# The S5 layer's parameter tables in a decoder trunk: products moved from GpSimd to VectorE, without the zero half, with 16 angles in place of 64

## The chip, the core and the metric

The kernel runs on one core of a Trainium2 chip. The metric is device time in microseconds (us), the median of the runs. Engines are named as in the profile: PE (TensorE, PEld is its weight load), DVE (VectorE), ACT (ScalarE), POOL (GpSimd), SP (SyncE, which only starts transfers here).

## What is computed

A trunk of two layers on 256 tokens of 1024 channels. Each layer is a SwiGLU feed-forward with a layer norm, a token mixer with a layer norm, a second feed-forward with a layer norm, and a gated embedding. The mixer of the first layer holds an S5 recurrence, and the change is in what is prepared for it:

```
lam_bar = jnp.exp(lam * dt)
b_bar = ((lam_bar - 1.0) / lam)[..., None] * lax.complex(b_re, b_im)
bu = jnp.einsum('blgp,gnp->blgn', ug, b_bar)
_, states = lax.associative_scan(linear_recurrence_combine, (a, bu), axis=1)
y = jnp.real(jnp.einsum('blgn,gpn->blgp', states, c)) + d_skip * ug
```

There are 64 groups of 16 channels, with 64 complex states each.

## The kernel before

**Feed-forward.** Four feed-forward blocks run, named f00, f01, f10 and f11. Each takes 11 chunks of 256 hidden columns. Weights come as units of 1 MB (wst, two buffers, started by SP). ACT casts each half of a unit to float32r (wh, L61), DVE subtracts to get the rest (wl, L63), and PE multiplies three times: x high with wh, x high with wl, x low with wh (L71 to L73). For a chunk, gate and up go into gu_f; ACT applies SiLU (sg_f, L204), DVE multiplies (L205), PE transposes (ht_f, L208), ACT and DVE split the result (hh_f L211, hl_f L212), and PE multiplies down into acc_f. At the end DVE starts the layer norm (r_ln, L124).

**S5 parameters.** They are computed during f00, in hooks between its chunks (`params`, L1308), from weights alone. First `s5_scalars` makes small tables of powers of the eigenvalue (s5lq, s5le, 128x32 each). Then there are eight batches of four pairs of groups. Two groups share the 128 partitions, 64 states each. The loaded B and C (s5m) have 32 columns for a pair, and half of them are zero, so that a product of the matrix with both groups' channels keeps the groups apart. A batch (`s5_params`):

- loads s5m, 256 KB;
- DVE makes B times its factor (s5tv, s5e, 6 operations of 128x128);
- POOL makes the products with three powers for E (6 operations of 128x384) and four powers for Q (6 of 128x512, into the packed tile s5pk);
- DVE and ACT make cosine and sine of 64 angles for each of 4 pairs (s5x, s5y: DVE 11 operations of 128x256, ACT two Sin);
- POOL starts the transfer of s5pk to DRAM (s5d);
- one hook later, in `rest`, PE transposes E (s5w, 8 transposes) and multiplies E with C (s5k, 16 matmuls), ACT copies both into s5pe and makes six block copies, DVE adds the skip weights (s5dd), POOL clears part of s5pe, and starts its transfer.

s5pk, s5pe and s5e have two buffers each. The mixer behind f00 reads all of it back from DRAM.

**Order.** Each engine runs its own queue in order. The order within a queue is made at build time by a scheduler that has its own estimates of durations; no table written by hand sets it. An instruction that waits holds up all behind it on its engine.

Of the kernel before, what the change touches and what calls it, by code (L numbers as in the profile page):

```python
# [114 lines left out]
def layer_norm(g, n, t, acc, coef, xT):  # L115
    """LN(ALPHA * x + ALPHA * coef * acc) of one token tile, from the scaled sum x + coef * acc."""
# [44 lines left out]
def run_tiles(g, ps, xT, tile_major=False):  # L161
    """x @ w for the next 512 columns of weights into one accumulator a token tile."""
# [22 lines left out]
def ffn(g, name, ln, hooks=None):  # L185
    """SwiGLU, accumulated over chunks of 256 hidden columns, and the LN behind it."""
# [62 lines left out]
def ple_proj(g, i, pT):  # L249
    """p[i] @ ple_w_proj[i]."""  # L250
# [22 lines left out]
def ple(g, i, pp, out):  # L273
    """x + sigmoid(x @ ple_w_gate[i]) * pp; the last layer's goes out."""
# [64 lines left out]
def s5_scalars(g):  # L339
    """What every state of the S5 layer needs: B's factor, powers of the discrete eigenvalue, its phase over  # L340
    four steps as a fraction of a turn in two parts, and its decay over four steps."""
# [5 lines left out]
    LE = g.s5c.tile([P, 2, 3, 32], F32, tag="le", name="s5le")  # L347
# [85 lines left out]
def s5_params(g, b):  # L433
# [72 lines left out]
    def rest():  # L506
        pk = g.s5p.tile([P, PACK_PE], F32, tag="s5pe", name=f"s5pe_{b}", bufs=2)
        W = pk[:, 0:1024].rearrange("p (a q c) -> p a q c", a=2, q=NP)
        T = pk[:, 1024:1536].rearrange("p (q c) -> p q c", q=NP)
        for i in range(2):  # L510
            tp = g.ps.tile([P, NP, P], F32, tag="tr", name=f"s5w_{b}_{i}", bufs=2)
            for q in range(NP):
                nc.tensor.transpose(tp[:, q, :], E[:, i, q, :], g.ident)
            nc.scalar.copy(W[:, i], tp)
        kp = g.ps.tile([P, NP, 32], F32, tag="tr", name=f"s5k_{b}", bufs=2)
        for q in range(NP):
            nc.tensor.matmul(kp[:, q, :], E[:, 0, q, :], Cr[:, q, :], start=True, stop=False)
            nc.tensor.matmul(kp[:, q, :], E[:, 1, q, :], nCi[:, q, :], start=False, stop=True)
        nc.gpsimd.memset(T, 0.0)
        nc.scalar.copy(T[:, :, 96:128], kp)  # L520
# [8 lines left out]
        nc.gpsimd.dma_start(g.s5dram[b][:, 0:PACK_PE], pk)  # L529
# [4 lines left out]
def project(g, name, tile_major=False):  # L534
    """x @ w for the next 512 columns: one accumulator a token tile."""
# [5 lines left out]
def narrow_project(g, pool, src, name, tag=None):  # L541
    """A [1024, 16] product by channel: rows 0-15 and 16-31 of the result sum to it."""
# [20 lines left out]
def to_channels(g, src, cts, out_ps):  # L563
    """Transposes [tokens, channels] tiles: out_ps[:, i, :] holds channel tile cts[i] for all tokens."""
# [5 lines left out]
def softplus_terms(g, v, shape, pool, name):  # L570
    """log1p(exp(-|v|)) of a small tile, accurate for small results too."""
# [17 lines left out]
def s5_inputs(g, pool, U, c):  # L589
    """Half of u, laid out [(4 steps, 2 groups, 16 channels), pair of groups, 64 chunks of steps]."""  # L590
# [28 lines left out]
def s5_batch(g, pool, U, G, b):  # L619
    """Four pairs of groups: states at the ends of chunks of four steps by a scan in the rotating frame, then  # L620
    the outputs."""
# [19 lines left out]
    def turn(src, name, out, ops):  # L641
        """The products with cos and sin, and out = (c0 op s1, c1 op s0)."""
# [22 lines left out]
def s5_half_out(g, G, c, yh, yl):  # L665
    """GELU of half of the channels, by channel, and its parts."""
# [22 lines left out]
def s5_outputs(g, pool, yT, yh, yl):  # L689
    """The gated outputs by channel, in two parts."""  # L690
# [788 lines left out]
```

## Time and profile before

| | us |
|---|---|
| runs of the kernel, median (lowest to highest) | 1315.52 (1308.86 to 1315.69) |
| profiled execution, first to last instruction (its span, the only time given of it) | 1321.4 |
| f00, from its first matmul to the first layer norm operation | 254.3 |
| f01 and f10, the same stretch | 180.3 each |

The profiled execution's span is 5.9 us above the median of the runs, which don't carry the profiler. A stage's row gives the stretch, its length, and then the busy time and the count of instructions of PE, PEld, DVE, ACT and POOL; PEclk is the granted clock of PE, 1.00 being 2.4 GHz and 0.50 being 1.2 GHz. A group's row gives count, busy time, mean duration, and behind the second bar the idle time just before them with what ended it. Durations of neighbours on one engine overlap by some 0.05 us, since the next starts before the last has written back; busy time counts an overlap once.

### The profile page before, as it was taken

What the parts mean: (1) busy time and instruction counts of PE and PEld (TensorE: products, weight loads), DVE (VectorE), ACT (ScalarE), POOL (GpSimd) and SP (SyncE); (2) the same over time, 40 slices, a digit from 0 to 9 for tenths busy, and PEclk for the clock granted to TensorE, in tenths of its full rate; (3) what the DMA queues carried; (4) which work ended last, traced back from release to release, by engine and by line L of the source; (5) the groups of instructions that cost most, each with busy time, mean ns of one, the idle gap of its engine ahead of it and who ended that gap; (6) DMA issues with size and microseconds to landing.
All of it is one profiled execution on the core that took longest, in us unless ns stands there. A gap on an engine that the chain in (4) does not pass through costs nothing.

```text
span 1321.4 us, 15959 instructions
## 1 busy us (share of the span) xinstructions
PE 1243.2 (94%) x6026; PEld 1024.8 (78%) x6026; DVE 887.9 (67%) x1230; ACT 625.5 (47%) x965; POOL 382.2 (29%) x307
## 2 busy tenths in 40 slices
PE   7899887999989799999999999999889999999998
PEld 6677666877878687788888788888667787888886
DVE  6999797577875875655557655555649867555566
ACT  6445444456454653444453554444355544444434
POOL 0557776544536652000000000000366650000000
PEclk9899898999998899999999999999988999999999
DMA  7556546765753144655563655555443135655542
GB/s 277 173 201 229 179 182 229 276 231 168 258 193 138 59 142 159 230 197 182 190 216 105 250 191 191 191 182 201 146 131 124 65 135 177 209 188 191 191 159 96
DMA packets 39932, 238.98 MB, mean 181 GB/s; under 512 B 4624, under 2 KB 5296, under 8 KB 16176
## 3 DMA queue, kind: packets, MB, share of 16 engines
q1 hardware_dynamic: 30960, 206.58, 44.9%
q10 hardware_dynamic: 5952, 15.66, 3.3%
q0 software_dynamic: 2944, 15.73, 3.1%
q8 instruction: 47, 0.77, 0.2%
q14 instruction: 29, 0.24, 0.1%
HBM read 223.27 MB, written 14.68 MB: 180 GB/s over the span
## 4 chain that ended last, share of the span: by engine, by line
PE 61%; DVE 19%; DMA 7%; POOL 5%; issue 4%; ACT 4%; ACTq 0%; DVEq 0%; POOLq 0%; SPq 0%
PE gu_f L73 9%; PE gu_f L72 9%; PE gu_f L71 9%; DVE wl L63 5%; PE acc_f L71 5%; PE acc_f L73 5%; PE acc_f L72 5%; DMA wst<-in_wall_dram 4%; DMA s5m<-in_s5bc_dram 2%; ACT wh L61 2%; PE ht_f L208 1%; PE acc_ab L73 1%; PE acc_ab L71 1%; PE acc_ab L72 1%; POOL wl L63 1%
## 5 line engine op out<-in xcount | busy, mean ns | idle before, releaser
L63 DVE TENSOR_TENSOR wl<-wst,wh 128x1024 fp32r<-128x1024 f32 (+1 forms) x332 | 424.3, 1293 | 279.6 <-ACT wh L61 272.3
L61 ACT CAST wh<-wst 128x1024 fp32r<-128x1024 f32 (+1 forms) x378 | 386.0, 1045 | 309.8 <-PE gu_f L73 101.6
L63 POOL TENSOR_TENSOR wl<-wst,wh 128x1024 fp32r<-128x1024 f32 x46 | 120.5, 2621 | 310.7 <-ACT wh L61 310.7
L73 PE MATMUL acc_f<-wh,hl_f 128*128 128x512 f32 x352 | 140.0, 402 | 12.9 <-DVE hl_f L212 12.9
L71 PE MATMUL acc_f<-wh,hh_f 128*128 128x512 f32 x352 | 139.8, 398 | 3.7 <-ACT hh_f L211 3.6
L72 PE MATMUL acc_f<-wl,hh_f 128*128 128x512 f32 x352 | 140.0, 398 | 0.0
L82 POOL TENSOR_TENSOR rs_r_ln<-rs_w_ln,mhalf 128x1 f32<-128x1 f32 x12 | 11.3, 944 | 425.5 <-DVE rs_w_ln L80 425.5
L73 PEld LDWEIGHTS acc_f<-wh,hl_f 128*128 128x128 f32 x352 | 68.0, 193 | 29.7 <-DVE hl_f L212 15.6
L71 PEld LDWEIGHTS acc_f<-wh,hh_f 128*128 128x128 f32 x352 | 67.5, 192 | 18.6 <-ACT hh_f L211 5.0
L71 PE MATMUL gu_f<-wh,xh_in 128*128 128x512 f32 x176 | 73.1, 420 | 8.0 <-ACT wh L61 6.1
L72 PEld LDWEIGHTS acc_f<-wl,hh_f 128*128 128x128 f32 x352 | 67.5, 192 | 14.0
L73 PE MATMUL gu_f<-wh,xl_in 128*128 128x512 f32 x176 | 72.4, 411 | 0.0
L72 PE MATMUL gu_f<-wl,xh_in 128*128 128x512 f32 x176 | 72.1, 411 | 0.0
L71 PE MATMUL gu_f<-wh,xh_ab 128*128 128x512 f32 x176 | 69.8, 397 | 0.5 <-ACT xh_ab L110 0.5
L71 PE MATMUL gu_f<-wh,xh_cd 128*128 128x512 f32 x176 | 69.8, 397 | 0.5 <-ACT xh_cd L110 0.5
L73 PE MATMUL gu_f<-wh,xl_ab 128*128 128x512 f32 x176 | 69.0, 392 | 0.7 <-DVE xl_ab L111 0.7
L71 PE MATMUL gu_f<-wh,xh_ple 128*128 128x512 f32 x176 | 69.7, 396 | 0.0
L73 PE MATMUL gu_f<-wh,xl_cd 128*128 128x512 f32 x176 | 68.9, 392 | 0.7 <-DVE xl_cd L111 0.7
L73 PE MATMUL gu_f<-wh,xl_ple 128*128 128x512 f32 x176 | 69.0, 392 | 0.0
L72 PE MATMUL gu_f<-wl,xh_cd 128*128 128x512 f32 x176 | 68.8, 391 | 0.2 <-DVE wl L63 0.2
L72 PE MATMUL gu_f<-wl,xh_ab 128*128 128x512 f32 x176 | 68.8, 391 | 0.1
L72 PE MATMUL gu_f<-wl,xh_ple 128*128 128x512 f32 x176 | 68.6, 390 | 0.0
(475 smaller groups left out, 2704.6 us busy)
## 6 DMA issues: line engine op xcount, KB each, us to landing
wst<-in_wall_dram SPq DMA_DIRECT2D x185, 1024.0 KB, 4.9
s5d<-s5pk POOLq DMA_DIRECT2D x8, 896.0 KB, 4.5
s5d<-s5pe POOLq DMA_DIRECT2D x8, 768.0 KB, 4.3
row<-in_lnr_dram SPq DMA_DIRECT2D x12, 512.0 KB, 5.8
W<-s5d ACTq DMA_DIRECT2D x8, 512.0 KB, 5.4
Q<-s5d ACTq DMA_DIRECT2D x8, 512.0 KB, 5.4
tab<-s5d ACTq DMA_DIRECT2D x8, 384.0 KB, 4.1
wst<-in_wall_dram SPq DMA_DIRECT2D x4, 512.0 KB, 6.2
```

Source lines behind the costliest of these rows:

```text
L61: ops = [nc.scalar.copy(wh[:, c], src[:, c])]
L63: ops.append(eng.tensor_tensor(wl[:, c], src[:, c], f32(wh[:, c]), op=ALU.subtract))
L71: nc.tensor.matmul(out, xh, wh, start=first, stop=False)
L72: nc.tensor.matmul(out, xh, wl, start=False, stop=False)
L73: nc.tensor.matmul(out, xl, wh, start=False, stop=last)
L82: nc.gpsimd.tensor_tensor(r, w, g.mhalf.broadcast_to([P, n]), op=ALU.pow)
L208: nc.tensor.transpose(tp[:, k, :], sg[:, k * P:(k + 1) * P], g.ident)
```

## The change

- Zeros: B and C are stored without their zero half, 16 columns for a pair in place of 32, in two loads of 512 KB (s5m, one buffer), the first started by ACT, the second by POOL.
- Products: all complex products are made by DVE in tiles of 128x256 (L507, four for a complex product) and one sum of 128x512 (L508), three such groups for a batch: for E, for Q, and for the angles. POOL multiplies nothing.
- Angles: a table of 64 angles is the product of 8 fine and 8 coarse ones. So cosine and sine are taken of 16 angles, for sixteen pairs at once, in `s5_half`, which runs twice and also makes B times its factor.
- Spreading: ACT writes the narrow E and Q into the blocks of the wide tiles with two multiplications by a column of ones and zeros each (L522; s5eb, s5pk).
- Buffers: s5pk and s5pe have one buffer, and E and Q share one (tag s5e). s5pe is cleared once.
- Text in quotes at the functions' heads is taken out; this changes no instruction.

```diff
-    m = g.s5p.tile([P, 4, NP, 32], F32, tag="s5m", name=f"s5m_{b}", bufs=2)
-    src = g.s5bc[b].rearrange("p (a q c) -> p a q c", a=4, q=NP)
...
-    cmul(nc.vector, (tv[:, 0], tv[:, 1]), *e3, Br, Bi, *(bc(v[:, ps], 2, 32) for v in g.s5B))
-    tg = g.s5p.tile([P, 2, NP, 4, 32], F32, tag="s5t", name=f"s5t_{b}")
-    Ev = E.rearrange("p a q (s c) -> p a q s c", s=4)
-    cmul(nc.gpsimd, (tg[:, 0, :, 0:3], tg[:, 1, :, 0:3]), Ev[:, 0, :, 0:3], Ev[:, 1, :, 0:3],
-         bc(e3[0], 2, 3), bc(e3[1], 2, 3), powers(LE, 0), powers(LE, 1))
-    cmul(nc.gpsimd, (tg[:, 0], tg[:, 1]), Q[:, 0], Q[:, 1], bc(Cr, 2, 4), bc(nCi, 2, 4), powers(LQ, 0), powers(LQ, 1),
-         neg=True)
...
+def s5_load(g, h):
+
+    m = g.s5p.tile([P, 5, HP, 16], F32, tag="s5m", name=f"s5m_{h}", bufs=1)
+    (g.nc.gpsimd if h else g.nc.scalar).dma_start(m[:, 0:4], g.s5bc[h].rearrange("p (a q c) -> p a q c", a=4, q=HP))
+    return m
...
+    nc.scalar.mul(m[:, 3], m[:, 3], -1.0)
+    nc.scalar.mul(m[:, 4], m[:, 2], -1.0)
...
+    for i in range(2):
+        nc.vector.tensor_tensor(p0[:, i], Br2[:, i], bc(g.s5B[0][:, ps], 2, 16), op=mul)
+        nc.vector.tensor_tensor(p1[:, i], Br2[:, i], bc(g.s5B[1][:, ps], 2, 16), op=mul)
...
+    for j in range(2):
+        nc.scalar.mul(cb[:, :, :, j, :], m[:, 2:4], g.cst("half")[:, j:j + 1])
...
+    nc.scalar.activation(z[:, 2], x, AF.Sin, scale=TWO_PI)
+    nc.scalar.activation(y, x, AF.Sin, scale=0.5 * TWO_PI)
...
+    t0 = g.s5p.tile([P, 2, 256], F32, tag="s5t0", name=f"s5t0_{b}", bufs=1)
+    t1 = g.s5p.tile([P, 2, 256], F32, tag="s5t1", name=f"s5t1_{b}", bufs=1)
+
+    def cmul(out, a, br, bi, shape):
+
+        for t, at, v in ((t0, 0, br), (t1, 1, bi)):
+            for i in range(2):
+                nc.vector.tensor_tensor(t[:, i].rearrange(shape[0], **shape[1]), a(at, i), v, op=mul)
+        nc.vector.tensor_tensor(out, t0, t1, op=add)
...
+    E = g.s5p.tile([P, 2, 256], F32, tag="s5e", name=f"s5e_{b}", bufs=1)
+    cmul(E, lambda at, i: bc(e3[:, (1 - at) + i, hs], 2, 4), powers(LE, 0), powers(LE, 1), by_power)
+    Eb = g.s5p.tile([P, 2, NP, P], F32, tag="s5eb", name=f"s5eb_{b}", bufs=2)
+    pk = g.s5p.tile([P, PACK - PACK_PE], F32, tag="s5pk", name=f"s5pk_{b}", bufs=1)
+
+    def by_pairs(src, dst):
+        for j in range(2):
+            nc.scalar.mul(dst.rearrange("p (n j c) -> p n j c", j=2, c=16)[:, :, j, :],
+                          src.rearrange("p a (n c) -> p (a n) c", c=16), g.cst("half")[:, j:j + 1])
+
+    by_pairs(E, Eb.rearrange("p a q c -> p (a q c)"))
+    Q = g.s5p.tile([P, 2, 256], F32, tag="s5e", name=f"s5q_{b}", bufs=1)
+    cmul(Q, lambda at, i: bc(c3[:, at + i, hs], 2, 4), powers(LQ, 0), powers(LQ, 1), by_power)
+    by_pairs(Q, pk[:, 768:1792])
+    fine, coarse = (lambda i: bc(z[:, i, hs, 0:8], 2, 8)), (lambda i: bc(z[:, i, hs, 8:16], 3, 8))
+    cmul(pk[:, 0:512].rearrange("p (a n) -> p a n", a=2), lambda at, i: fine((1 - at) + i), coarse(1), coarse(2),
+         ("p (q a b) -> p q a b", dict(q=NP, a=8)))
```

In the queues this stands as follows. POOL's queue before, one batch's products and transfers (the batch whose tiles end in 1139 and 1138):

```order
L455 TENSOR_TENSOR s5t_1149<-s5e_1139,s5le 128x4x96
L456 TENSOR_TENSOR s5t_1149<-s5e_1139,s5le 128x4x96
L457 TENSOR_TENSOR s5e_1139<-s5t_1149 128x4x96
L458 TENSOR_TENSOR s5t_1149<-s5e_1139,s5le 128x4x96
L459 TENSOR_TENSOR s5t_1149<-s5e_1139,s5le 128x4x96
L463 TENSOR_TENSOR s5e_1139<-s5t_1149 128x4x96
L455 TENSOR_TENSOR s5t_1149<-s5m_1136,s5lq 128x512
L456 TENSOR_TENSOR s5t_1149<-s5nci_1140,s5lq 128x512
```

POOL's queue now, from the third batch's packed tile (s5pk_943) to the fifth's:

```order
L534 MEMSET s5pk_943 128x4
L535 DMA s5d_89<-s5pk_943 128x1792
L439 DMA s5m_1144<-in_s5bc_dram 128x1024
L534 MEMSET s5pk_1125 128x4
L558 DMA s5d_88<-s5pe 128x1536
L535 DMA s5d_90<-s5pk_1125 128x1792
L534 MEMSET s5pk_1343 128x4
L558 DMA s5d_89<-s5pe 128x1536
```

The products have left this queue; only small clears and the starts of transfers stay, among them the second load of s5m.

ACT's queue at the start of f00 before, from the second unit's cast (wh_1_155) to the first chunk's SiLU (sg_f_0):

```order
L61 CAST wh_1_155<-wst_148 128x1024
L370 ACT_TABLE_LOAD
L370 ACTIVATE s5tmp<-lc 128x32
L61 CAST wh_0_236<-wst_233 128x1024
L374 ACTIVATE s5tmp<-s5tmp 128x32
L61 CAST wh_1_240<-wst_233 128x1024
L204 ACT_TABLE_LOAD
L204 ACTIVATE sg_f_0_0_211<-gu_f_0_0_129 128x256
```

The same place now, behind that cast, a table load and one small operation:

```order
L450 ACTIVATE s5m_211<-s5m_211 128x256
L451 ACTIVATE s5m_211<-s5m_211 128x256
L463 ACTIVATE s5cb_548<-s5m_211,cs 128x32x16 x2
L377 ACTIVATE s5tmp<-s5tmp 128x32
L61 CAST wh_0_240<-wst_237 128x1024
L385 ACT_TABLE_LOAD
L385 ACTIVATE s5tmp<-s5tmp 128x32
L386 ACTIVATE s5tmp<-s5tmp 128x32
L61 CAST wh_1_244<-wst_237 128x1024
L387 ACTIVATE s5tmp<-s5tmp,lc 128x32
L204 ACT_TABLE_LOAD
L204 ACTIVATE sg_f_0_0_215<-gu_f_0_0_129 128x256
```

Four operations that need the first load of s5m (L450 to L463) and one more table load now stand ahead of the first SiLU.

DVE's queue now in the heaviest chunk, where two batches' products (s5t_2, s5t_3) lie around the chunk's own work (wl, hl_f, sg_f):

```order
L507 TENSOR_TENSOR s5t_2_934<-s5m_211,s5lq 128x256 x2
L507 TENSOR_TENSOR s5t_2_935<-s5m_211,s5lq 128x256 x2
L508 TENSOR_TENSOR s5q_946<-s5t_2_934,s5t_2_935 128x512
L63 TENSOR_TENSOR wl_0_1021<-wst_1018,wh_0_1020 128x1024
L507 TENSOR_TENSOR s5t_2_934<-s5z_555 128x256 x2
L507 TENSOR_TENSOR s5t_2_935<-s5z_555 128x256 x2
L63 TENSOR_TENSOR wl_1_1025<-wst_1018,wh_1_1024 128x1024
L508 TENSOR_TENSOR s5pk_943<-s5t_2_934,s5t_2_935 128x512
L212 TENSOR_TENSOR hl_f_3_1_797<-ht_f_3_1_793,hh_f_3_1_796 128x256
L205 TENSOR_TENSOR sg_f_4_1_972<-sg_f_4_1_972,gu_f_4_1_801 128x256
```

The twelve products and three sums of a batch have come in between the feed-forward's operations; the chains of angle operations on s5x and s5y are gone from all but two places.

## Rows read from the trace of the kernel before

**Rows 1.** Windows f00, f01: stretch, length, busy by engine, PEclk, DMA share, GB/s.

```profile
6.10:260.40 254.30, 223.42 (x1012) 181.71 (x1013) 212.82 (x330) 119.64 (x227) 152.78 (x134) 0.93 0.62 222
524.40:704.70 180.30, 179.20 (x809) 146.97 (x810) 100.72 (x123) 83.56 (x114) 0.99 (x1) 1.00 0.57 198
```

**Rows 2.** Groups of PE in f00, with idle time ahead of them.

```profile
L73 PE MATMUL acc_f<-wh,hl_f 128*128 128x512 f32 x82 | 34.9, 441 | 12.9 <-DVE hl_f L212 12.9
L513 PE MATMUL s5w<-cs,s5e 128*128 128x128 f32 x64 | 10.1, 295 | 6.3 <-DVE hl_f L212 6.3
L208 PE MATMUL ht_f<-cs,sg_f 128*128 128x128 f32 x44 | 8.4, 284 | 6.1 <-DVE sg_f L205 6.1
```

**Rows 3.** Windows of f00 with GpSimd idle or at work, and one at low clock.

```profile
30.00:53.00 23.00, 23.00 (x105) 19.07 (x104) 19.95 (x53) 10.21 (x16) 8.34 (x7) 1.00 0.64 223
53.00:80.00 27.00, 21.64 (x90) 17.48 (x89) 26.79 (x36) 9.26 (x15) 24.02 (x19) 0.87 0.48 171
86.50:97.00 10.50, 10.50 (x52) 8.86 (x51) 9.25 (x19) 4.06 (x9) 1.11 (x2) 0.84 0.88 314
60.00:62.00 2.00, 1.56 (x5) 1.37 (x6) 2.00 (x3) 0.00 (x0) 1.18 (x1) 0.50 0.03 8
```

**Rows 4.** Groups of DVE in f00.

```profile
L63 DVE TENSOR_TENSOR wl<-wst,wh 128x1024 fp32r<-128x1024 f32 x65 | 96.4, 1491 | 12.4 <-ACT wh L61 12.1
L490 DVE TENSOR_SCALAR s5y<-s5y 128x256 f32<-128x256 f32 x16 | 13.4, 838 | 0.3
...
L111 DVE TENSOR_TENSOR xl_in<-xin,xh_in 128x512 fp32r<-128x512 f32 x4 | 2.8, 688 | 6.5 <-ACT xh_in L110 6.5
```

**Rows 5.** Timeline of DVE, 98 to 110 us; GpSimd starts a batch at 100.

```profile
99.44 0.28 DVE L490 TENSOR_SCALAR s5y<-s5y 128x256 f32<-128x256 f32 x1
...
101.25 0.41 DVE L500 TENSOR_TENSOR s5y<-s5y 128x256 f32<-128x256 f32 x1
...
101.79 1.21 DVE L63 TENSOR_TENSOR wl<-wst,wh 128x1024 fp32r<-128x1024 f32 x1
...
108.61 2.03 DVE L63 TENSOR_TENSOR wl<-wst,wh 128x1024 fp32r<-128x1024 f32 x1
```

**Rows 6.** Groups of GpSimd in f00: first and last of 12 groups of products.

```profile
L457 POOL TENSOR_TENSOR s5e<-s5t 128x384 f32<-128x384 f32 x8 | 13.3, 1666 | 0.6
...
L463 POOL TENSOR_TENSOR s5e<-s5t 128x384 f32<-128x384 f32 x8 | 9.6, 1203 | 0.5
```

**Rows 7.** Timeline of PE: one batch's s5w and s5k.

```profile
209.25 0.60 PE L513 MATMUL s5w<-cs,s5e 128*128 128x128 f32 x4
209.68 0.31 PE L517 MATMUL s5k<-s5m,s5e 128*128 128x32 f32 x2
...
211.39 0.48 PE L71 MATMUL gu_f<-wh,xh_in 128*128 128x512 f32 x1
```

**Rows 8.** Groups of ACT in f00.

```profile
L514 ACT COPY s5pe<-s5w 128x512 f32<-128x512 f32 x16 | 9.1, 586 | 6.0 <-PE s5w L513 6.0
...
L499 ACT ACTIVATE s5y<-s5x 128x256 f32<-128x256 f32 x8 | 3.3, 411 | 25.4 <-DVE s5x L491 25.4
```

**Rows 9.** Timeline of all engines at the start of f00.

```profile
6.36 0.42 ACTq L1293 DMA_DIRECT2D lc<-in_cols_dram  x1
...
14.89 1.28 ACT L370 ACT_TABLE_LOAD   x1
...
19.74 0.66 ACT L204 ACTIVATE sg_f<-gu_f 128x256 f32<-128x256 f32 x2
...
20.76 0.44 PE L208 MATMUL ht_f<-cs,sg_f 128*128 128x128 f32 x2 [0.78 <-DVE sg_f L205]
```

**Rows 10.** Transfers: kind, count, size, median us from issue to landing.

```profile
s5d<-s5pe POOLq DMA_DIRECT2D x8, 768.0 KB, 4.3
...
wst<-in_wall_dram SPq DMA_DIRECT2D x4, 512.0 KB, 6.2
...
lc<-in_cols_dram ACTq DMA_DIRECT2D x1, 117.5 KB, 8.1
```

More of the change, by code (lines that the diff above doesn't have):

```diff
@@ L488, in turn @@
+    nc.vector.tensor_tensor(dd[lo], bc(g.ident[lo, 96:128], 1, HP), bc(g.cols("s5d")[lo, ps], 2, 32), op=mul)
+    fh, fl, u4 = g.s5f
+    cidx = bc(g.cst("cidx"), 1, HP)
+    x = g.s5p.tile([P, HP, 16], F32, tag="s5x", name=f"s5x_{h}", bufs=1)
+    y = g.s5p.tile([P, HP, 16], F32, tag="s5y", name=f"s5y_{h}", bufs=1)
+    z = g.s5p.tile([P, 3, HP, 16], F32, tag="s5z", name=f"s5z_{h}", bufs=1)
     def turn(dst, src, tmp):
@@ L491, in turn @@
         nc.vector.tensor_tensor(dst, src, tmp, op=sub)
-    nc.vector.tensor_tensor(x, cidx, steps(fh), op=mul)
+    nc.vector.tensor_tensor(x, cidx, bc(fh[:, ps], 2, 16), op=mul)
     turn(x, x, y)
-    nc.vector.tensor_tensor(y, cidx, steps(fl), op=mul)
+    nc.vector.tensor_tensor(y, cidx, bc(fl[:, ps], 2, 16), op=mul)
     nc.vector.tensor_tensor(x, x, y, op=add)
     turn(x, x, y)
-    nc.scalar.activation(sinT, x, AF.Sin, scale=TWO_PI)
+    nc.scalar.activation(z[:, 2], x, AF.Sin, scale=TWO_PI)
@@ L499, in s5_params, with powers @@
     nc.scalar.activation(y, x, AF.Sin, scale=0.5 * TWO_PI)
+    nc.scalar.mul(z[:, 0], z[:, 2], -1.0)
     nc.vector.tensor_tensor(y, y, y, op=mul)
-    nc.vector.tensor_scalar(cosT, y, -2.0, 1.0, op0=mul, op1=add)
-    nc.scalar.copy(dec, steps(u4))
+    nc.vector.tensor_scalar(z[:, 1], y, -2.0, 1.0, op0=mul, op1=add)
+    return m[:, 2:5], e3, cb, dd, z
+def s5_params(g, b, half):
+    nc = g.nc
+    mul, add, sub = ALU.mult, ALU.add, ALU.subtract
+    c3, e3, cb, dd, z = half
+    ps = slice(NP * b, NP * b + NP)
+    hs = slice(NP * (b % 4), NP * (b % 4) + NP)
+    t0 = g.s5p.tile([P, 2, 256], F32, tag="s5t0", name=f"s5t0_{b}", bufs=1)
[5 more added lines that the diff above has]
+        nc.vector.tensor_tensor(out, t0, t1, op=add)
+    def powers(L, i):
+        return bc(L[:, i, :, ps].rearrange("p t q -> p q t"), 3, 16)
+    LE, LQ = g.s5L
+    by_power = ("p (q t c) -> p q t c", dict(q=NP, t=4))
+    E = g.s5p.tile([P, 2, 256], F32, tag="s5e", name=f"s5e_{b}", bufs=1)
[13 more added lines that the diff above has]
+         ("p (q a b) -> p q a b", dict(q=NP, a=8)))
+    dec = pk[:, 512:768].rearrange("p (q c) -> p q c", q=NP)
+    nc.scalar.copy(dec, bc(g.s5f[2][:, ps], 2, 64))
@@ L506, in rest @@
     def rest():
[L507 to L509 removed]
+        pe = g.s5pe
+        W = pe[:, 0:1024].rearrange("p (a q c) -> p a q c", a=2, q=NP)
+        T = pe[:, 1024:1536].rearrange("p (q c) -> p q c", q=NP)
         for i in range(2):
@@ L512, in rest @@
             for q in range(NP):
-                nc.tensor.transpose(tp[:, q, :], E[:, i, q, :], g.ident)
+                nc.tensor.transpose(tp[:, q, :], Eb[:, i, q, :], g.ident)
             nc.scalar.copy(W[:, i], tp)
         kp = g.ps.tile([P, NP, 32], F32, tag="tr", name=f"s5k_{b}", bufs=2)
+        cv = cb.rearrange("p a q j c -> p a q (j c)")
         for q in range(NP):
[L517 to L520, printed above, removed]
+            for i in range(2):
+                nc.tensor.matmul(kp[:, q, :], Eb[:, i, q, :], cv[:, i, hs.start + q, :], start=i == 0, stop=i == 1)
         lo = slice(96, 128)
-        dd = g.s5p.tile([P, NP, 32], F32, tag="s5dd", name=f"s5dd_{b}")
-        nc.vector.tensor_tensor(dd[lo], bc(g.ident[lo, 96:128], 1, NP), bc(g.cols("s5d")[lo, ps], 2, 32), op=mul)
-        nc.vector.tensor_tensor(T[lo, :, 96:128], T[lo, :, 96:128], dd[lo], op=add)
+        nc.scalar.copy(T[0:96, :, 96:128], kp[0:96])
+        nc.vector.tensor_tensor(T[lo, :, 96:128], kp[lo], dd[lo, hs], op=add)
         for t in range(3):
@@ L1239, in mixer_cd @@
         out_project(g, "cd", parts, ln, 1.0 / ALPHA, tail=2)
-CST = {"ident": 128, "incl": 128, "strict": 128, "mask3": 384, "cidx": 64, "levels": 448, "fold": 16}
+CST = {"ident": 128, "incl": 128, "strict": 128, "mask3": 384, "cidx": 16, "levels": 448, "fold": 16, "half": 2}
 COLS = {"conv": 80, "ssdw": 8, "bglu": 8, "s5v": 96, "s5d": 32, "halfpi": 1, "lb": 8, "glab": 2}
@@ L1305, in tile_trunk, with first @@
         g.s5p, g.s5c = s5p, s5c
-        rest = []
+        rest, half, loaded = [], [], []
+        def first():
+            load_constants()
+            loaded.append(s5_load(g, 0))
+            g.s5pe = s5c.tile([P, PACK_PE], F32, tag="s5pe", name="s5pe")
+            nc.gpsimd.memset(g.s5pe[:, 1024:1536], 0.0)
         def params(b):
@@ L1311, in params @@
             if b < NB:
-                rest.append(s5_params(g, b))
-        hooks = {-1: load_constants, 0: lambda: s5_scalars(g), NB + 2: load_x}
+                if b % 4 == 0:
+                    half[:] = [s5_half(g, b // 4, loaded[b // 4])]
+                rest.append(s5_params(g, b, half[0]))
+            if b == 3:
+                loaded.append(s5_load(g, 1))
+        hooks = {-1: first, 0: lambda: s5_scalars(g), NB + 2: load_x}
         for b in range(NB + 1):
@@ L1426, in layout @@
     s5v = np.concatenate([states(d["s5_lambda_re"][0]), states(d["s5_lambda_im"][0]), states(ldt)], axis=1)
[L1427 to L1432 removed]
+    bcs = np.stack([d["s5_b_re"][0], d["s5_b_im"][0], d["s5_c_re"][0].transpose(0, 2, 1),
+                    d["s5_c_im"][0].transpose(0, 2, 1)])
+    bcs = bcs.reshape(4, 2, HP, 2, 64, 16).transpose(1, 3, 4, 0, 2, 5).reshape(2, P, 4 * HP * 16)
     s5d = np.zeros((P, 32), np.float32)
```

63 lines of the change are left out of this document (20 added, 43 removed).

## Prediction, made before the changed kernel was run

> **What bounds the kernel now.** The change touches only f00, so the first view is that of the stages. f00 takes 254.3 us from its first matmul to its first layer norm operation, f01 with the same 792 large matmuls takes 180.3 [rows 1]; f10 agrees with f01. In f01 PE is busy all the time at full clock, while in f00 it stands idle for 254.3 - 223.4 = 30.9 us and its clock averages 0.93. So f01 is what the feed-forward costs when PE is the bound, and 74 us of f00 are S5's.
>
> The groups of PE tell what it waits for: the largest idle times end on DVE, at hl_f (12.9 and 6.3 us) and at sg_f (6.1) [rows 2]. The windows tell why DVE is late [rows 3]. From 53 to 80 us GpSimd is busy for 24.0 of 27 us, DVE for 26.8, and PE is idle for 5.4. From 30 to 53, with GpSimd busy for 8.3 of 23, and from 86.5 to 97, with 1.1 of 10.5, PE has no idle time, though DVE is busy 87% and 88% of the time.
>
> Last the durations. With GpSimd idle, wl takes 1.21 us, a DVE operation of 128x256 takes 0.41 with two tensors and 0.28 with a constant; some us later, with GpSimd's products running, wl takes 2.03 [rows 5]. Over f00 the mean of wl is 1.49, and that of L490 0.84 [rows 4]. DVE is stretched by GpSimd's products, falls behind, and PE waits for it.
>
> **The change, part by part.** Neighbours on DVE overlap by some 0.05 us, so in a sum of busy time I count an operation 0.05 shorter than its row.
>
> *DVE.* f01 gives the feed-forward's own part unstretched, 100.7 us [rows 1]. What S5 adds before, at the unstretched prices of [rows 5]: each batch has 6 operations of 128x256 with two tensors (0.36), 5 with a constant (0.23), 6 of 128x128 and 2 of 32x128 (0.23 at most), together 5.2 us, so 41.6 for eight. The 59 small operations of s5_scalars (128x32) I take at 8 us, and 13.6 at most (0.23 each). Then 212.8 - 100.7 - 41.6 - 8 = 62.5 us of DVE's busy time in f00 are stretch.
>
> Afterwards each batch has 12 products of 128x256 (0.36) and 3 sums of 128x512 (0.69 for that size [rows 4], so 0.64), 4.3 + 1.9 = 6.2 us, so 50 for eight; the two halves have 24 operations with two tensors and 10 with a constant, 10.9; two of 32x512 at 0.64, 1.3; eight additions at 0.36, 2.9; s5_scalars 8. That is 73, and DVE's busy time becomes 100.7 + 73 = 174 us, 39 less. Of these, trading the stretch for the moved products gives 62.5 - 50 = 12.5, and fewer angles and larger operations give 26.5. The unknown is whether the products, which read tables spread out by repetition, run at 0.41. The old operations that did (cidx times phase, the 128x128 ones) argue for it. The upper bound is the slowest mean in [rows 4], 0.84: 96 times 0.43 is 41 us more. I take 0.41, since no GpSimd product is left to stretch them.
>
> The Trainium skill, Perfetto Trace Analysis, section "Optimizing Scalar/DVE Operations", speaks against this part: GpSimd and VectorE share a read port of SBUF, so moving operations between the two might not help. By that sentence the move would be worth nothing and the 26.5 us of the angles would be all that DVE gains; by the rows it is worth 12.5 us more. The rows here agree with the shared port and show which way the trade goes.
>
> *GpSimd.* It loses all twelve groups of products of f00, 8 operations each, between 13.3 and 9.6 us a group [rows 6]. Its clears and transfer starts remain.
>
> *PE.* The same 8 transposes and 16 matmuls for a batch: 209.25 to 211.39 is 0.43 for four transposes and 1.71 for sixteen matmuls, so 2.57 a batch, 20.6 in all [rows 7]. The floor of f00 is 180.3 + 20.6 = 200.9 us.
>
> *ACT.* It gains 32 spreads of 128x512 at 0.59 [rows 8], 18.9, and about as many small operations as it loses: 119.6 [rows 1] becomes 138 of some 220 us. That is not a bound as a sum. Its waits for Sin's argument (25.4 us ahead of L499 [rows 8]) come from eight chains of DVE; two remain. But a spread waits for DVE with the casts of weights queued behind it.
>
> *The start.* Here the change adds a wait. Before, a table load at 14.89, and the SiLU at 19.74 releases PE at 20.76 [rows 9]. Now four operations on s5m come first, then one more table load. The s5m load goes out on ACT's queue behind lc, which starts at 6.4 [rows 9] and takes 8.1 us to land, so to 14.5; a transfer of 512 KB takes 6.2 [rows 10] while sharing. I put its landing at 17.5, between 16.4 (no wait) and 20. Behind it stand 2 x 0.42 + 2 x 0.59, small ones 0.22 + 0.22 + 0.22 + 0.33, two casts 1.04 each, two table loads 1.28 each and the SiLU 0.38: 8.0 us. DVE's multiplication adds 0.4, so PE's transpose starts at 25.9 in place of 20.76, 5.2 us later; between 4.1 and 8 by the bounds. PE stands behind that transpose, and nothing covers the wait: PE was busy without a gap from there to 53 us. After a wait of 5.4 us before, PE ran at half clock for 5.3 us (0.50 from 60 to 62 [rows 3]), which costs half of it, 2.6. The start costs 7.8 us more than before, besides the 3.0 that f00's first 48 matmuls lose already (6.13 us to 20.76 - 0.78 [rows 9], against 48 times 180.3 / 792).
>
> *Single buffers.* The next batch's copy into s5pe waits until the transfer of the last has landed, 4.3 us [rows 10]. In ACT's queue four casts, two spreads and two to four small operations lie between, 6.5 us or more, but for the last batch, with some 2.8. So I cost it at nothing but a wait of 2 us there, on ACT, while PE has 38 matmuls left before it needs the result, 8.7 us. If ACT ran without its casts it would cost up to 4.3 a batch. s5pk waits likewise, with a chunk between.
>
> *The second load.* s5m has one buffer, so POOL starts the second load when the fourth batch's Q products are made, and ACT negates part of it (L450) ahead of hh_f_4. Some 6.2 us to land [rows 10] stand against some 6 us of PE work between: 0 to 6 us of wait, counted below.
>
> *Remaining waits.* Busy windows without GpSimd had none, so the low bound is 0. The heaviest chunk holds two batches: six wl, four small ones and 12.4 us of S5 are some 21 us of DVE against 19 of PE. I count one wait of some 3 us each for that chunk, the second load, the chain of Sin and the end, and take 11.6, a little below the 12.9 that PE waited ahead of L73 [rows 2]; the high bound is all of the 30.9 again.
>
> **The sum.** 200.9 + 3.0 + 7.8 + 11.6 = 223.3 us for f00. The other way, DVE's 174 plus the 41.5 us that it was idle before plus the start's 7.8, gives 223. So 254.3 - 223.3 = 31 us are gained, and nothing behind f00 gives them back: the mixer's first matmuls wait for f00's layer norm, and S5's tables are ready by then. The profiled span of 1321.4 becomes 1290.4; the median of the runs, 5.9 below, becomes 1315.5 - 31 = **1284 us**.
>
> **Rivals.**
>
> - *ACT's queue takes back more* (0.20). The start at its upper bound and 2 to 3 us of waits for spreads and single buffers in each batch: 10 to 24 us less gained, 1294 to 1309. For it: eight more operations a batch go back and forth between DVE and ACT, and E and Q share one buffer. Against it: the scheduler has put other work between each pair.
> - *Nearly all waits go* (0.08). Stage of 205 to 210: 1266 to 1272. For it: the two windows without GpSimd. Against it: the start.
> - *The relief doesn't come* (0.07). Products at 0.84 give DVE its 41 us back, and DVE bounds f00 as before: 1309 to 1322. This is the page's caution in its strong form. For it: DVE has more operations than before (342 against 330) in the same queue. Against it: the same shapes at 0.41 when GpSimd is idle.
> - *Slower* (0.05). ACT, at each batch, waits for DVE at the two pairs of spreads and at s5pe, with weight casts behind, and DVE waits for those casts. It decides from some 5.9 us of idle PE a batch on: 47 us in eight, with the start, are more than the 53.4 us between f00 now and its floor. Then 1322 to 1335.
>
> **The numbers.** The forecast has 0.60, with 1271 to 1294 as its own range (start 4.1 to 8, remaining waits 2 to 20, price of the products up to 0.5). The range of 1268 to 1308 leaves out the last two rivals and the best part of the second. Some 0.5% (6.6 us) is what a measurement of this kernel can tell from no change. Faster by more is the forecast and the first two rivals, 0.88; within it 0.07; slower 0.05.
>
> **What would show it.** In the profile after: wl in f00 at a mean near 1.22; L507 at 0.41 and L508 at 0.69; DVE busy for 174 us in f00; the first ht_f near 26 us, with half clock behind it; f00 near 223 us with PE's idle time below 22; the stages behind f00 as long as before. It is wrong if L507 runs well above 0.41, if PE's waits end on ACT in every batch, or if the mixer gets longer.

## The result, and the profile after

The changed kernel takes 1280.07 us (median of 4 runs, 1277.89 to 1280.53) against 1314.53 (4 runs, one more than behind the 1315.52 of the first table) for the kernel before: ratio 0.972, 95% interval 0.970 to 0.975. The forecast was 1284. The profiled execution is one of the four runs: it took 1277.89 us, with a span of 1276.1.

The windows of f00, from its first matmul to its first layer norm operation, and its two parts; the columns are those of [rows 1].

```profile
6.00:221.20 215.20, 209.40 (x1014) 172.83 (x1015) 166.21 (x342) 140.68 (x252) 12.46 (x26) 0.99 0.71 254
6.00:30.00 24.00, 19.75 (x68) 14.73 (x69) 17.36 (x46) 17.38 (x29) 0.00 (x0) 0.93 0.78 284
30.00:221.20 191.20, 189.65 (x948) 158.09 (x947) 148.86 (x297) 123.31 (x224) 12.46 (x26) 1.00 0.70 250
```

The stage is 39.1 us shorter than in [rows 1], PE's idle time is 5.8 us where it was 30.9, and DVE is busy for 166.2 us instead of 212.8. From 30 us on PE is idle for 1.6 us in all, at full clock. Groups of DVE in f00:

```profile
L63 DVE TENSOR_TENSOR wl<-wst,wh 128x1024 fp32r<-128x1024 f32 x65 | 78.8, 1221 | 25.2 <-ACT wh L61 24.9
L507 DVE TENSOR_TENSOR s5t<-s5e,s5le 128x256 f32<-128x256 f32 x32 | 11.6, 418 | 0.1
L507 DVE TENSOR_TENSOR s5t<-s5z 128x256 f32<-128x256 f32 x32 | 11.5, 419 | 0.1
L508 DVE TENSOR_TENSOR s5q<-s5t,s5t 128x512 f32<-128x512 f32 x8 | 5.5, 690 | 3.2 <-ACT s5eb L522 3.2
```

Groups of PE in f00, with the idle time ahead of them:

```profile
L73 PE MATMUL acc_f<-wh,hl_f 128*128 128x512 f32 x83 | 31.7, 399 | 0.2 <-DVE hl_f L212 0.2
L208 PE MATMUL ht_f<-cs,sg_f 128*128 128x128 f32 x44 | 8.6, 278 | 4.2 <-DVE sg_f L205 4.2
```

wl is at 1.22 us in place of 1.49 [rows 4], the products at 0.42 and the sums at 0.69. The wait on hl_f of [rows 2] has gone from 12.9 us to 0.2. What is left stands at one place, the start. From ACT's timeline, with PE's transpose in the last row:

```profile
14.87 1.28 ACT L373 ACT_TABLE_LOAD   x1
...
16.30 0.40 ACT L450 ACTIVATE s5m<-s5m 128x256 f32<-128x256 f32 x1
...
19.31 1.28 ACT L385 ACT_TABLE_LOAD   x1
...
22.13 1.28 ACT L204 ACT_TABLE_LOAD   x1
23.43 0.66 ACT L204 ACTIVATE sg_f<-gu_f 128x256 f32<-128x256 f32 x2
...
24.32 0.44 PE L208 MATMUL ht_f<-cs,sg_f 128*128 128x128 f32 x2 [4.24 <-DVE sg_f L205]
```

Work on S5 and a third table load stand ahead of the SiLU, which starts 3.7 us later than in [rows 9]. Behind the wait the granted clock is low: PE spends part of these two windows at the lower of its two levels (1.2 and 2.4 GHz), so that their means are 0.64 and 0.74:

```profile
24.40:27.00 2.60, 2.60 (x9) 2.12 (x10) 2.60 (x11) 1.83 (x3) 0.00 (x0) 0.64 0.84 325
27.00:30.00 3.00, 3.00 (x12) 2.35 (x12) 1.39 (x4) 0.65 (x2) 0.00 (x0) 0.74 0.53 131
```

The two profiled spans differ by 45.3 us, 39.1 of it in f00. The remaining 6.2 us lie in code that the change doesn't touch: behind f00 the execution before takes 1321.4 - 260.4 = 1061.0 us, the one after 1276.1 - 221.2 = 1054.9. Over all profiled executions below this rest lies between 1051.7 and 1060.6 us, with no relation to f00. So a few us between two medians are no evidence on f00; its own window is, and the verdicts below go by it. Two kernels were profiled twice, and their two windows of f00 differ by 0.7 and 2.4 us.

### The profile page after: what moved, and what is told of

It reads as the page before. It is cut to its first block, busy times and chain, and to the rows that moved or that the text cites. A ratio compares the mean times of both kernels' runs of the same rounds, so it can differ in the third digit from the quotient of the medians.

```text
span 1276.1 us, 15873 instructions
## 1 busy us (share of the span) xinstructions
PE 1226.4 (96%) x6026; PEld 1014.6 (80%) x6026; DVE 838.9 (66%) x1242; ACT 646.0 (51%) x990; POOL 239.8 (19%) x201
## 4 chain that ended last, share of the span: by engine, by line
PE 59%; DVE 12%; ACT 3%; DMA 2%; issue 2%; POOL 1%; ACTq 0%; DVEq 0%; POOLq 0%; SPq 0%
PE gu_f L73 9%; PE gu_f L72 9%; PE gu_f L71 9%; PE acc_f L73 5%; PE acc_f L71 5%; PE acc_f L72 5%; DVE wl L63 2%; DMA wst<-in_wall_dram 2%; PE acc_ab L73 1%; PE acc_ab L72 1%; PE acc_ab L71 1%; PE ht_f L208 1%; DVE rw L682 1%; ACT wh L61 1%; DVE U L643 1%
## 5 line engine op out<-in xcount | busy, mean ns | idle before, releaser
L63 DVE TENSOR_TENSOR wl<-wst,wh 128x1024 fp32r<-128x1024 f32 (+1 forms) x332 | 404.1, 1232 | 290.4 <-ACT wh L61 284.0
L71 PE MATMUL acc_f<-wh,hh_f 128*128 128x512 f32 x352 | 137.1, 391 | 1.3 <-ACT hh_f L211 1.2
L73 PE MATMUL acc_f<-wh,hl_f 128*128 128x512 f32 x352 | 136.4, 392 | 0.2 <-DVE hl_f L212 0.2
L204 ACT ACTIVATE sg_f<-gu_f 128x256 f32<-128x256 f32 x88 | 33.6, 383 | 70.3 <-PE gu_f L73 70.1
```

Source lines behind the costliest of these rows:

```text
L63: ops.append(eng.tensor_tensor(wl[:, c], src[:, c], f32(wh[:, c]), op=ALU.subtract))
L71: nc.tensor.matmul(out, xh, wh, start=first, stop=False)
L73: nc.tensor.matmul(out, xl, wh, start=False, stop=last)
L204: nc.scalar.activation(sg, ps[t][:, 0:256], AF.Silu)
```

## Experiments

Theory 1 is the prediction's: GpSimd's products slow DVE while they run beside it, DVE falls behind, PE waits. Its rivals are the number of DVE operations (angles, halves), and the chains of dependent work (Sin, or E and Q coming late from GpSimd).

**e1_noprod: before, with GpSimd's products left out.**

```diff
-    cmul(nc.gpsimd, ... E ...)
-    cmul(nc.gpsimd, ... Q ...)
+    nc.gpsimd.memset(E[:, :, :, 0:96], 0.5)
+    nc.gpsimd.memset(pk[:, 768:1792], 0.5)
```

> The kernel before with GpSimd's 12 products and sums of each batch left out (two clears on GpSimd stand in their place, so the tables E and Q hold a constant); all else as before, the 64 angles and the wide form too. Theory 1, GpSimd's products stretch DVE and DVE makes PE wait: DVE's busy time in f00 falls from 212.8 us by the 62.5 us that I worked out as stretch, to some 150; wl has a mean near 1.22; f00 falls from 254.3 to 205 to 215 us, so the run to 1267 to 1277 us. Theory 2, the time came from the number of DVE operations and the eight chains of Sin: wl stays above 1.4, f00 stays above 240, the run above 1300.

1269.97 us, ratio 0.965 (0.962 to 0.968). Its window of f00:

```profile
6.00:212.39 206.39, 206.22 (x1012) 172.28 (x1013) 148.34 (x330) 121.17 (x227) 29.07 (x50) 1.00 0.75 273
```

Groups of its DVE, wl and an operation with a constant:

```profile
L63 DVE TENSOR_TENSOR wl<-wst,wh 128x1024 fp32r<-128x1024 f32 x65 | 78.7, 1220 | 29.5 <-ACT wh L61 29.1
...
L488 DVE TENSOR_SCALAR s5y<-s5y 128x256 f32<-128x256 f32 x16 | 5.4, 340 | 0.3
```

The same 330 operations of DVE that took 212.8 us take 148.3: 64.5 us were stretch, where the prediction had worked out 62.5. PE has no wait. The window also gives the floor of f00, 206 us, and splits what f00 loses before the change: 30.7 us more idle time and 17.2 us more busy time at a lower clock.

**e9_unread: the same, with the products made for nobody.** It separates running beside DVE from being waited for.

The two clears of e1_noprod stay, and beside them:

```diff
-    cmul(nc.gpsimd, ..., Ev[:, 0, :, 0:3], Ev[:, 1, :, 0:3], ...)
+    cmul(nc.gpsimd, ..., tg[:, 0, :, 0:3], tg[:, 1, :, 0:3], ...)
-    cmul(nc.gpsimd, ..., Q[:, 0], Q[:, 1], ...)
+    cmul(nc.gpsimd, ..., tg[:, 0], tg[:, 1], ...)
```

> The kernel of e1_noprod (E and Q hold a constant, cleared on GpSimd), with GpSimd's 12 wide products and sums of each batch made all the same, from the same operands, into their own scratch tile, which nothing else reads. Theory 1 (the products slow DVE by running beside it): DVE's busy time goes back from 148 to 205 to 215 us, wl to a mean of 1.45 to 1.5, f00 from 206 to 240 to 255, the run 1300 to 1318. Theory 2 (PE waited because E and Q came late from GpSimd, which takes 17 us a batch): nothing waits for these, so f00 stays at 206 to 215, the run 1267 to 1277, whatever DVE's durations.

1319.47 us, ratio 1.003 (1.001 to 1.005): all of the gain of e1 is gone again, as theory 1 had it (the run 1.5 us above its range, DVE's busy time, wl at 1.49 and f00 within theirs). Its window of f00:

```profile
6.09:256.89 250.80, 219.48 (x1012) 178.74 (x1013) 207.49 (x331) 118.28 (x227) 160.22 (x146) 0.95 0.62 224
```

Results that no engine reads cost what the needed ones cost. The constants in E and Q still come from GpSimd's queue, as clears behind the last batch's products, but no wait of PE in this stage ends on GpSimd: of its 31.3 us idle, 26.7 end on DVE and 4.7 on ACT. So late E and Q are out as the main cause. How the two engines meet is to be seen in this run's timeline, of which the rows of DVE and GpSimd stand here:

```profile
106.53 0.41 DVE L205 TENSOR_TENSOR sg_f<-sg_f,gu_f 128x256 f32<-128x256 f32 x1
106.53 1.01 POOL L457 TENSOR_TENSOR s5t<-s5t 128x384 f32<-128x384 f32 x1
106.86 1.77 DVE L63 TENSOR_TENSOR wl<-wst,wh 128x1024 fp32r<-128x1024 f32 x1
...
110.14 0.95 POOL L475 MEMSET s5pk<- 128x1024 f32 x1
110.51 0.42 DVE L497 TENSOR_TENSOR s5y<-cs,s5sc 128x256 f32<-128x256 f32 x1
...
112.34 1.08 POOL L455 TENSOR_TENSOR s5t<-s5m,s5lq 128x512 f32<-128x512 f32 x1
112.49 1.09 DVE L492 TENSOR_SCALAR s5y<-s5y 128x256 f32<-128x256 f32 x1
113.38 1.13 POOL L456 TENSOR_TENSOR s5t<-s5nci,s5lq 128x512 f32<-128x512 f32 x1
113.61 1.19 DVE L493 TENSOR_TENSOR s5x<-s5x,s5y 128x256 f32<-128x256 f32 x1
```

wl, beside products most of the time, takes 1.77 us instead of 1.22. From 112.3 us on the engines keep step: a DVE operation that takes 0.28 or 0.42 us alone takes 1.09 and 1.19, as long as the GpSimd operation beside it. But sg_f, one of whose operands is in PSUM, keeps its 0.41 beside a product, and a DVE operation with two SBUF operands keeps 0.42 beside a clear, which reads nothing. So here a short DVE operation that meets a product takes as long as the product, whatever its own size. Over the whole of f00 the price is lower, since not every DVE operation meets one: the 64.5 us of stretch are 0.67 us for each of the 96 products.

**e2_dveprod and e7_dveprod_again: the move alone.** The kernel before, wide products with their zero half, 64 angles, and one word changed twice:

```diff
-    cmul(nc.gpsimd, ...
+    cmul(nc.vector, ...
```

> The kernel before with one change: the same 12 products and sums of each batch, in the wide form with the zero half, on DVE. Theory 1 (stretch): six operations of 128x384 at some 0.50 us and six of 128x512 at 0.64 are 6.8 us a batch, 55 in all, against 62.5 of stretch: DVE busy 205, wl near 1.22, f00 by DVE's sum 242 to 250, the run 1303 to 1311. So the move alone gives little, and the halved products give the rest. Theory 2 (GpSimd's work cost DVE nothing that a move would give back): DVE busy 255 to 268, f00 290 to 309, the run 1350 to 1370.

1274.41 us, ratio 0.969 (0.966 to 0.972): far below what either theory had given, and as fast as the whole change or faster. Its window of f00:

```profile
6.00:213.23 207.23, 206.66 (x1013) 172.34 (x1014) 195.58 (x427) 120.93 (x227) 20.59 (x38) 1.00 0.73 265
```

DVE is busy for 195.6 of 207.2 us and PE is idle for 0.6. DVE's busy time falls by 17 us, where the expectation's numbers gave 7.5 (the products cost DVE 195.58 - 148.34 = 47.2 us, not 55), but f00 falls by 47. The expectation for f00 had added DVE's old idle time, 41.5 us, to its busy time; here it idles for 11.6. The second run stood beside the kernel after:

> The kernel after itself, to stand beside the two others of this call on the same chip: 1278 to 1281 us.

> The kernel before with its wide products on DVE, once more beside the kernel after. Theory: the smaller tables, fewer angles and spreads of the change give f00 nothing once the products are off GpSimd, since PE is the bound in both, and the change's start costs 7 to 8 us: so this one is 5 to 9 us faster than the kernel after, 1271 to 1276 us. Rival: the 5.7 us between the two medians so far is spread between runs, mostly of the mixers: within 2 us of the kernel after.

The kernel after: 1280.15 us (1276.42 to 1282.16), f00 215.9. The move alone: 1270.61 (1269.10 to 1271.55), f00 209.6; ratios 0.972 (0.969 to 0.974) and 0.965 (0.963 to 0.967). Their windows of f00, in this order:

```profile
5.94:221.80 215.86, 210.45 (x1014) 173.65 (x1015) 166.25 (x342) 140.67 (x252) 12.46 (x26) 0.98 0.70 253
5.67:215.27 209.60, 207.46 (x1013) 172.05 (x1014) 195.75 (x426) 120.42 (x227) 18.60 (x37) 1.00 0.73 264
```

The theory held against its rival: the rest of the change costs time, 6 to 8 us of f00. The medians differ by 9.5 us, a little more than the 5 to 9 forecast. In these two profiles f00 differs by 6.3 us and the code behind it by 6.9, which is the spread of that code seen above.

**e8_dve213: as much DVE work as before, unstretched.**

```diff
+        for _ in range(times):      # 2 for E, 1 elsewhere
             eng.tensor_tensor(t[0], ar, br, op=mul)
             eng.tensor_tensor(t[1], ai, bi, op=mul)
...
-    cmul(nc.gpsimd, ...             # E and Q
+    cmul(nc.vector, ...             # E with times=2, and Q
```

> The kernel before with its wide products on DVE, and the four multiplications of E made twice in each batch (the second time over the same values), 32 more DVE operations of 128x384 at some 0.50 us: DVE is busy for some 212 us in f00, as it was before the change (212.8), but with nothing of it stretched by GpSimd. Theory 1 (GpSimd's products make DVE late in bursts, in which PE waits, and DVE idles between them): f00 is DVE's busy time and a tenth of it at most, 214 to 228 us, the run 1281 to 1295. Theory 2 (what counts is DVE's busy time, as my prediction's second way of summing had it, with the 41.5 us that DVE was idle before): f00 250 to 256, the run 1312 to 1320.

1284.52 us, ratio 0.977 (0.974 to 0.980). Its window of f00:

```profile
5.62:227.34 221.72, 213.47 (x1016) 174.91 (x1017) 209.44 (x457) 120.22 (x225) 18.56 (x37) 0.98 0.68 249
```

DVE's busy time is within 3.4 us of that of [rows 1], and f00 is 32.6 us shorter. So DVE's sum alone didn't set f00 before. In [rows 3] the stretch comes in bursts, in which DVE is busy 26.8 of 27 us and PE waits, and between them DVE has time to spare that nothing can use. In windows of 12 us from 42 to 222 us DVE is busy for 7.2 to 11.9 us before the change and for 10.2 to 12.0 in e8: spread more evenly, its work fills 94% of the stage.

**e3_narrow_pool: after, with the narrow E and Q products on GpSimd.**

```diff
-    cmul(E, ...)                      # 4 products, 1 sum on VectorE
+    cmul_pool(E, ...)                 # 4 products, 2 sums of 128x256 on GpSimd
-    cmul(Q, ...)
+    cmul_pool(Q, ...)
```

> The kernel after with E's and Q's products back on GpSimd in the narrow form (12 operations of 128x256 a batch); the rotation tables' products stay on DVE. Theory 1 (stretch in proportion to GpSimd's work: 62.5 us for some 137 us of GpSimd before, 0.46 for each): some 75 us of GpSimd stretch DVE by 34, as much as the 34 us of operations that leave it, so DVE is busy for 160 to 170 as in the kernel after (166), wl at a mean of 1.35 to 1.45, PE still the bound: f00 215 to 222, the run 1278 to 1287. Rival: while GpSimd runs, DVE falls behind however little it has to do; f00 225 to 240, the run 1290 to 1305.

1290.14 us, ratio 0.980 (0.978 to 0.983): the rival's f00 and time, though DVE's busy time (158) and wl's mean (1.345) are about those of theory 1. Its window of f00:

```profile
5.90:233.72 227.82, 212.37 (x1014) 175.35 (x1015) 157.94 (x262) 140.36 (x252) 101.85 (x122) 0.97 0.68 240
```

A piece of its DVE timeline:

```profile
77.95 3.50 DVE L507 TENSOR_TENSOR s5t<-s5z 128x256 f32<-128x256 f32 x3
81.37 0.73 DVE L475 TENSOR_SCALAR s5y<-s5x 128x256 f32<-128x256 f32 x1
82.02 0.41 DVE L205 TENSOR_TENSOR sg_f<-sg_f,gu_f 128x256 f32<-128x256 f32 x1
```

PE's timeline at that place:

```profile
82.48 0.80 PE L71 MATMUL gu_f<-wh,xh_in 128*128 128x512 f32 x1 [5.33 <-DVE sg_f L205]
```

DVE is busy for 8 us less than after the change, and f00 is 12.6 us longer. Three rotation products that take 0.42 us alone take 3.5 together, and the sg_f for which PE stands idle is queued behind them.

This run doesn't separate that from a second effect: E and Q come later, and ACT's spreads wait for them, 12.5 and 6.9 us in all, with weight casts and SiLUs queued behind. The longest of these waits comes ahead of the piece above:

```profile
67.19 3.69 POOL L522 TENSOR_TENSOR s5e<-s5e,s5tg 128x256 f32<-128x256 f32 x1
67.40 1.42 DVE L507 TENSOR_TENSOR s5t<-s5z 128x256 f32<-128x256 f32 x4
...
69.08 1.21 DVE L63 TENSOR_TENSOR wl<-wst,wh 128x1024 fp32r<-128x1024 f32 x1
...
70.91 1.34 ACT L531 ACTIVATE s5eb<-s5e,cs 128x512 f32<-128x512 f32 x2 [7.51 <-POOL s5e L522]
```

Here it is GpSimd that is held up: its sum takes 3.69 us, against 0.72 at 80.44 us, while DVE's operations beside it keep their lengths. How much of the 12.6 us is stretch of DVE and how much ACT's wait stays open.

**e4_64_angles: after, with 64 angles.** The 16 angles and their products are replaced by the old code of a batch.

> The kernel after with 64 angles in each batch, as before, in place of 16 and their products; all else as after. The prediction put 26.5 of DVE's 39 us to fewer angles and larger operations: by it DVE is busy for 185 to 193 us, f00 takes 225 to 240, the run 1290 to 1305. Rival: the rotation products that replace the angles (four of 128x256 and one sum a batch, 2.1 us) eat most of that, an angle chain of 3.3 us a batch goes for 2.1 + 0.8, so DVE has only 3 to 4 us more, 170, and f00 stays at 215 to 219 unless the chain of Sin, eight times in place of two, makes PE wait; the run 1278 to 1284.

1281.77 us, ratio 0.974 (0.971 to 0.977), not to be told from the kernel after (0.972). Its window of f00:

```profile
6.10:224.75 218.65, 209.57 (x1013) 172.70 (x1014) 170.24 (x369) 143.37 (x262) 12.60 (x26) 0.99 0.69 250
```

DVE gains 4.0 us by fewer angles, not some twenty. The rival's arithmetic held. f00 is some 3 us longer than after the change, little more than two profiles of one kernel differ by; PE is idle for 9.1 us in place of 5.8.

**e5_start: after, without the wait at the start.**

```diff
-    nc.scalar.activation(dt, ldt, AF.Exp)
+    behind(g, nc.scalar.activation(dt, ldt, AF.Exp), g.silu)       # the SiLUs of chunk 0
-    nc.scalar.mul(m[:, 3], m[:, 3], -1.0)
+    behind(g, nc.scalar.mul(m[:, 3], m[:, 3], -1.0), g.silu0)      # and the one of m[:, 4]
```

> The kernel after with one edit: ACT's first Exp of s5_scalars and its two negations of s5m are queued behind the second SiLU of chunk 0 in place of ahead of the first. Theory: the start's wait (4.2 us ahead of the first ht_f, with PE at half clock behind it: PE is busy for 3.2 us longer in f00 than in the run without products) goes, nothing else moves: the first ht_f before 20 us with less than 0.8 us of wait, f00 from 215.2 to 207 to 209 us, the run from 1280 to 1272 to 1274. Rival: the S5 chain then starts later and its casts meet the later chunks, so waits of the same size come back between 30 and 60 us: f00 213 to 218, the run 1278 to 1283.

1275.32 us (1268.66 to 1278.23), ratio 0.968 (0.965 to 0.971). Its window of f00:

```profile
6.07:216.06 209.99, 207.38 (x1014) 171.02 (x1015) 166.32 (x343) 140.25 (x252) 12.47 (x26) 1.00 0.72 260
```

The first transpose in its PE timeline:

```profile
20.50 0.44 PE L208 MATMUL ht_f<-cs,sg_f 128*128 128x128 f32 x2 [1.10 <-DVE sg_f L205]
```

f00 is 5.2 us shorter than in the first profile of the kernel after and 5.9 than in the second: 3.1 us of wait and 2 to 3 of PE's busy time at low clock. The theory held, with the stage 1 us and the run 1.3 us longer and the first ht_f some 0.5 us later than it had said. The waits that the rival expected between 30 and 60 us didn't come: from there to the end PE is idle for 1.5 us in all, as in the kernel after.

**e10_spreads_twice: more load on ACT.**

```diff
-        for j in range(2):
+        for j in (0, 1, 0, 1):
             nc.scalar.mul(dst[..., j, :], src, half[:, j:j + 1])
```

> The kernel after with each of ACT's 32 spreads made twice (the second over the same values): 21.5 us more of ACT, from 140.7 to 162 of 215. Theory (ACT is no bound as a sum, and the spreads lie beside PE's work): f00 215 to 220 us, the run 1278 to 1285. Rival of the prediction (ACT's queue takes back: a spread waits for DVE with weight casts queued behind it): 1.4 us more in each of 16 places, with DVE's next operation waiting for the spread: f00 225 to 237, the run 1290 to 1302.

1280.91 us, ratio 0.973 (0.970 to 0.975): no change against the kernel after. Its window of f00:

```profile
6.10:221.60 215.50, 209.49 (x1014) 172.60 (x1015) 165.90 (x342) 159.90 (x284) 12.51 (x26) 0.99 0.71 254
```

The DVE group behind the first spreads of a batch:

```profile
L508 DVE TENSOR_TENSOR s5q<-s5t,s5t 128x512 f32<-128x512 f32 x8 | 5.5, 687 | 10.0 <-ACT s5eb L522 10.0
```

ACT takes 19.2 us more, DVE waits 10.0 us for spreads where it waited 3.2, and f00 is as long as in the kernel after.

## Why the prediction came out right, and where it was not

**What bounds f00: right, and shown.** e1 and e9 differ by GpSimd's products alone, and they carry 44 us of f00. The stretch of 62.5 us was 64.5.

**Which part of the change gives the time: wrong.** The step "trading the stretch for the moved products gives 12.5, and fewer angles and larger operations give 26.5" failed twice. In its bookkeeping, the five operations a batch that replace the angles (2.1 us, 16.6 in eight) were charged to the move; fewer angles are worth 4.0 us of DVE (e4). And what DVE's busy time loses is not what f00 gains: the move alone takes 17 us off DVE's busy time and 47 off f00 (e2), and everything else in the change takes another 29 off DVE and adds 6 to 8 to f00: PE is already the bound, so DVE's relief gives nothing, and the start costs. The time comes from the move, all of it.

**The second way of summing: wrong.** DVE's 174 plus the 41.5 us that it was idle gave 223, and so seemed to confirm the sum. The idle time is no constant: 11.6 us in e2, 12.3 in e8, 49.0 after the change. An agreement of two sums was taken for evidence; e2 and e8 show that DVE's old idle time can't be carried into a sum for another kernel.

**The terms of PE's sum.** Floor and old start, 203.9, measured as 206.4 (e1's f00); the 2.5 us between stay open. The start, 7.8: the first ht_f at 24.32 instead of 25.9, as s5m was there when ACT came to it (16.30, the "no wait" bound, against 17.5); the 8.4 us of work counted behind it took 8.0. With e5, the start costs 5 to 6. Remaining waits, 11.6: measured 5.8 - 4.2 = 1.6. This was the term most mis-sized. None of the four waits of some 3 us that I listed came. There were 0.8 us ahead of one acc_f on hh_f, which stood behind two spreads in ACT's queue, 0.25 on hl_f and some 0.5 elsewhere; the second load cost ACT 0.3 us. The low bound, 0, which the windows without GpSimd had spoken for [rows 3], was the better choice. So f00 took 215.2 instead of 223.3, nearer to the rival "nearly all waits go" than to the forecast.

**Why the total fitted better than the stage: luck.** f00 gained 39.1 us in the profiles against 31 forecast, but the medians differ by 34.5 only. The forecast went from a span to a median by taking off 5.9 us, as the kernel before seemed to have it. But the profiled execution before, with a span of 1321.4 us, is longer than each of its four timed runs (1315.69 at most), and behind f00 it is the longest of all that were profiled (1061.0). After the change the median lies 4.0 us above the profiled span. So the span was forecast 14.3 us too long (1290.4 against 1276.1), 8.1 of it in f00 and 6.2 behind it, and the step from span to median took some 10 of these back. How much of the difference lay in f00 of the timed runs stays open.

**The signs.** wl 1.22, L507 at 0.42, L508 at 0.69: as forecast. DVE busy 166 against 174. The spreads were under-sized, 0.72 us each against 0.59, 21.4 us in all; e10 shows that it made no difference. The single buffers cost ACT more than the 2 us forecast, 6.5 us of waits for the transfer of s5pk and 3.5 for that of s5pe, but no wait of PE ends there, and the spreads cost it the 0.8 us above at most. The rival "ACT's queue takes back more" is out: ACT could take another 19 us. The mixers are as long as before within what they vary by themselves.

**The Trainium skill's caution.** The rows come first: with products on GpSimd f00 takes 250.8 us, with none 206.4, with the same ones on DVE 207.2. The Trainium skill, Perfetto Trace Analysis, section "Optimizing Scalar/DVE Operations", says that moving work between the two might not help because they share a port; here the move was the whole gain, and the measurement decides. The Trainium skill, SBUF — State Buffer, section "Who interferes with whom", says that a DVE instruction with two SBUF inputs meets a GpSimd instruction that reads SBUF and not one that only writes, and one with at most one SBUF input, outside the modes that use both ports, meets neither. e9's timeline agrees: 1.19 us beside a product, 0.42 beside a clear, 0.41 for sg_f with its operand in PSUM. But L492 there has one SBUF operand and a constant, and beside a product it takes 1.09 us in place of 0.28; no row shows in which mode it ran.

## What to carry to other kernels

Price work on GpSimd by what it adds to the operations of DVE that run beside it (here 0.67 us for a product), not by GpSimd's own time: moving it onto a DVE that was 84% busy, stretch included, shortened the stage here. Judge an engine's load by windows, not by its sum, since bursts of it make others wait and the gaps between them are lost. When a change has several parts, run the smallest one alone: two words gave all of the gain, and the rest cost 6 to 8 us of f00, of which 5 to 6 come from what it queued ahead of the first SiLU (e5). The fastest version found is the kernel before with its products on DVE, 1270.6 us (0.965), not told apart with certainty from e5_start, 1275.3 (0.968).

## What the runs showed of the hardware

- The wait goes both ways: beside two-operand work of DVE that kept its lengths, one GpSimd sum of 128x256 took 3.69 us in e3, against 0.72 some 13 us later.
- DVE's short operations suffer most beside GpSimd's products: the one with a constant (128x256) has a mean of 0.84 us before [rows 4] and 0.34 in e1; wl goes from 1.22 to 1.49 only.
- How full DVE may be: in e2 it is busy for 94% of f00 and PE is idle for 0.6 us. In e8 it is 94% as well, but of a stage 14.5 us longer, in which PE is idle for 8.3. At 195.6 us of work DVE just kept up with PE here, at 209.4 it did not.
- A spread of 128x512 on ACT took 0.72 us, against 0.59 for the copy of the same size from PSUM [rows 8]. It differs in three ways, gaps in its output, a column to multiply by, and a source in SBUF; no run shows which of them costs the 0.13 us.
